# Decay matrices in four more places, first gram products together, inverse rows stored in one transfer

## The chip, the cores and the metric

The kernel runs on one core of one Trainium2 chip. The metric is the device time of one execution in microseconds (us); where several runs are given, their median. TensorE (PE) does the matrix products, VectorE (DVE), ScalarE (ACT) and GpSimd (POOL) the rest; SyncE (SP) issues nearly all DMA transfers. Each engine works through its own instructions in a fixed order.

## The reference

One layer of a diffusion backbone: a feed-forward block, then two mixers side by side (a neighbourhood attention and a bidirectional gated delta rule), then a second feed-forward block. The change lies in the delta rule, cut here to what matters:

```python
def gated_delta_chunks(q, k, v, g, beta, s0, with_output):
    # S_t = exp(g_t) (I - beta_t k_t k_t^T) S_{t-1} + beta_t k_t v_t^T,  o_t = S_t^T q_t
    k, v, g, beta = chunk(k), chunk(v), jnp.cumsum(chunk(g), axis=-1), chunk(beta)
    decay = jnp.exp(jnp.where(lower, g[..., :, None] - g[..., None, :], -jnp.inf))
    m = jnp.where(strict, jnp.einsum('...ik,...jk->...ij', k_beta, k) * decay, 0.0)
    uw = lax.linalg.triangular_solve(jnp.eye(GDN_CHUNK, dtype=m.dtype) + m, rhs,
                                     left_side=True, lower=True, unit_diagonal=True)
    ...
    def step(s, xc):
        v_new = xc[0] - jnp.einsum('...ck,...kv->...cv', xc[1], s)
        s_next = s * xc[3][..., None, None] + jnp.einsum('...ck,...cv->...kv', xc[2], v_new)
        return s_next, (jnp.einsum('...ck,...kv->...cv', xc[4], s)
                        + jnp.einsum('...cj,...jv->...cv', xc[5], v_new))
```

For each chunk of tokens there is a decay matrix `exp(g_i - g_j)` below the diagonal, the gram product of the keys times it, the inverse of one plus that matrix, and a scan that carries a state from chunk to chunk. The scores of queries against keys need the same decay matrix.

## The kernel before

The delta rule works on chunks of 128 tokens: two of context and four of latent tokens, forwards and backwards. A step `s` (0 to 5) handles one chunk of each direction, a pair `p` (0 or 1) two of the four heads, so one call handles four matrices at a time (index `m`). Steps go in groups `bi` of two: group 0 is steps 0 and 1 (context, no queries), group 1 steps 2 and 3, group 2 steps 4 and 5.

`gram(p, s, ...)` (lines 1106 to 1124) makes the decay matrices. Line 1110 loads the cumulated decays, broadcast over the partitions, into a tile `Dt`; line 1113 subtracts the column's value and adds the mask, one instruction a matrix; line 1114 takes the exponential on ACT. `Dt` is a tag with two buffers in the pool `gb_`, for twelve calls. Line 1119 makes `Bt`, gram product times decay times beta, and line 1120 stores it to DRAM (`bd`); where there are queries, line 1123 makes `At`. The products come from `products(p, s)`: group 0 takes them from PSUM (step 1 uses those of step 0), group 1 as well, and also stores them to DRAM (`kqd`, line 1094) for group 2, which loads them back (line 1098).

`base_inverse` (lines 1127 to 1153) inverts all 64 diagonal blocks of 32 x 32 of a group at once on DVE: lines 1138 to 1142 load the blocks from `bd` (two of four loads pass through `Ltr` and a copy on ACT), then 31 steps follow, each a product (line 1146, `bt`) and a sum (line 1147, `Xt`), each waiting for the one before. This is called the base chain below; there are three, one a group. A partition holds one block's columns of one parity. Lines 1150 to 1152 store the result to `rd` in four transfers. `inverse` (lines 1162 to 1226) loads it back as `T0` and `T1` (line 1168, two transfers), transposes on DVE (lines 1170, 1171) and joins the blocks to 128 x 128 inverses by small matrix products on PE (tile `pi`), with copies `Y`, `T6` and `Tt` on DVE and ACT between them. `scan_step` does a step of the scan; its products are in the tile `pc`, its sums on DVE are `r`, `vn`, `S`, and its output goes to one of the two tiles `oaccs`, written first at step 2.

What fills PE beside all this is the projection of the input: a fill is one column tile (24 matrix products of 128 x 512 into `pm`, lines 192 to 194), which needs its weights split on ACT (`wh`, line 137) and DVE (`wl`, line 139) and ends with a copy on ACT and a store (`spill`, lines 796 to 802). A fill comes in four pieces of six products. `turn(kind, i)` (line 1064) hands out a number of pieces from the table `RATE`, bound behind the last delta rule product: 2 after each gram of group 0, 3.9 after each product of group 1.

The program as written is not the order in which engines work: a scheduler with a simulated timeline places each engine's instructions, and `tc.issue_after(x)` keeps what it encloses behind instruction `x`. The sequence of the calls is this:

```python
    step(grams(0))
    base = grams(1)
    inv_of(0, 0)
    step(base, 4)
    inv_of(0, 1)
    step(base)
    scan_of(0, 0)
```

The attention's first loads (`att_load`: `qa`, `ka`, `kc`, `bias`, `va`, lines 1360 to 1367) go into the memory of `gb_` once that is closed, behind group 2's base chain in the program.

Of the kernel before, what the change touches and what calls it, by code (L numbers as in the profile page):

```python
# [13 lines left out]
ALU = mybir.AluOpType  # L14
# [4 lines left out]
P = 128  # L19
# [39 lines left out]
def body(ctx, tc, I, out, dbg=None):  # L59
    nc = tc.nc  # L60
    V, S, G, T = nc.vector, nc.scalar, nc.gpsimd, nc.tensor
# [15 lines left out]
    def tl(p, shape, tag, bufs=1, dt=F32):  # L77
        uid[0] += 1
        return p.tile(list(shape), dt, name=f"{tag}_{uid[0]}", tag=tag, bufs=bufs)
# [24 lines left out]
    marks = {}  # L104
# [461 lines left out]
    g = []  # L566
# [244 lines left out]
    beta = tl(gd, [P, 2, 6, 4], "beta")  # L811
# [252 lines left out]
    def turn(kind, i):  # L1064

        due[0] += RATE[kind][i]
        while due[0] >= 1:
            due[0] -= 1
            with tc.issue_after(last[0]):
                next(fills, None)  # L1070
# [9 lines left out]
    def products(p, s):  # L1080

        def one(n, a, o):
            if s == 1:
                return [kk01[p][:, m ^ 2] for m in range(4)]
            if s < 4:
                t = tl(pgq, [P, 4, P], "pq", 2)
                for m, (d, c, i) in enumerate(mats_of(s)):
                    mm(t[:, m, :], kT[2 * p + i][:, c], a[2 * p + i][:, c - o], start=True, stop=True)
                if s == 0:
                    kk01[p] = t  # L1090
                else:
                    u = tl(gb_, [P, 4, P], "kq", NKQ)
                    S.copy(u[:], t[:])
                    nc.sync.dma_start(kqd[n, s - 2, p], u[:].rearrange("p m c -> p (m c)"))
            else:
                t = tl(gb_, [P, 4, P], "kq", NKQ)
                for h in range(2):
                    nc.sync.dma_start(t[:, 2 * h:2 * h + 2].rearrange("p m c -> p (m c)"), kqd[n, 5 - s, p, :, 256 * (1 - h):256 * (2 - h)])
            return t
        yield one(0, kT, 0)  # L1100
        turn("g", s // 2)
        if s >= 2:
            yield one(1, qT, 2)
            turn("g", s // 2)

    def gram(p, s, bd, g):

        mats = mats_of(s)
        Dt = tl(gb_, [P, 4, P], "Dt", 2)
        nc.sync.dma_start(Dt[:], bass.AP(gcd.tensor, gcd.offset + (4 * s + 2 * p) * P, [[0, P], [24 * P, 2], [1, 2 * P]]))  # L1110
        for m, (d, c, i) in enumerate(mats):
            msk = cst[:, (C_MF if d == 0 else C_MB):][:, 0:P]
            V.scalar_tensor_tensor(Dt[:, m], Dt[:, m], gcum[:, d, s, 2 * p + i:2 * p + i + 1], msk, op0=ALU.subtract, op1=ALU.add)
        S.activation(Dt[:], Dt[:], AF.Exp)
        Bt, At = tl(gq, [P, 4, P], "Bt", NBT), None
        for n, t in enumerate(products(p, s)):
            if n == 0:
                for m, (d, c, i) in enumerate(mats):
                    V.scalar_tensor_tensor(Bt[:, m], t[m] if s == 1 else t[:, m], beta[:, d, s, 2 * p + i:2 * p + i + 1], Dt[:, m], op0=ALU.mult, op1=ALU.mult)
                nc.sync.dma_start(bass.AP(bd.tensor, bd.offset + g * MSTR, [[P, P], [4 * MSTR, 4], [1, P]]), Bt[:])  # L1120
            else:
                At = tl(gq, [P, 4, P], "At", NAT)
                V.tensor_tensor(At[:], t[:], Dt[:], ALU.mult)
        return Bt, At


    def base_inverse(bd, rd):


        L = tl(gb_, [P, 32, 32], "L")  # L1130
        tr = tl(gb_, [64, 32, 32], "Ltr")
        Xt = tl(gb_, [P, 16, 32], "Xt", 2)
        G.memset(Xt[:], 0.0)
        for q in range(4):
            G.memset(Xt[32 * q:32 * q + 32].rearrange("p c k -> p (c k)")[:, q % 2:512:34], 1.0)
        st = 32 * P + 32
        for q in range(4):
            dst = tr[32 * q:32 * q + 32] if q < 2 else L[32 * q:32 * q + 32]
            nc.sync.dma_start(dst, bass.AP(bd.tensor, bd.offset + (q // 2) * 8 * MSTR, [[st, 32], [P, 32], [1, 32]]))
        S.copy(L[0:64].rearrange("p r c -> p c r"), tr[:])  # L1140

        G.memset(L[:].rearrange("p r c -> p (r c)")[:, 0:1024:33], -1.0)
        for i in range(1, 32):
            c = (i + 1) // 2
            t = tl(gb_, [P, 16, 32], "bt")
            V.tensor_tensor(t[:, 0:c, 0:i + 1], L[:, i:i + 1, 0:i + 1].to_broadcast([P, c, i + 1]), Xt[:, 0:c, 0:i + 1], ALU.mult)
            V.tensor_reduce(Xt[:, 0:c, i], t[:, 0:c, 0:i + 1], AX, ALU.add, negate=True)
            if i % 4 == 0:
                yield
        for q in range(4):  # L1150
            nc.sync.dma_start(bass.AP(rd.tensor, rd.offset + (q // 2) * 32 * 1024 + (q % 2) * 32, [[1024, 32], [64, 16], [1, 32]]),
                              Xt[32 * q:32 * q + 32])
        yield


# [6 lines left out]
    def inverse(bi, st, rd, Bts):  # L1162


        T0 = tl(gq, [P, 8, 32], "T0", 2)
        T1 = tl(gq, [P, 8, 32], "T1", 2)
        for dst, d in ((T1, 0), (T0, 1)):
            nc.sync.dma_start(dst[:, 4 * d:4 * d + 4], bass.AP(rd.tensor, rd.offset + (st + 8 * d) * 4096, [[32, P], [2 * 4096, 4], [1, 32]]))
        fl = lambda t, m: t[:, m:m + 4].rearrange("p m c -> p (m c)")
        V.transpose(fl(T0, 0), fl(T1, 0))  # L1170
        V.transpose(fl(T1, 4), fl(T0, 4))
        blk = [slice(32 * b, 32 * b + 32) for b in range(4)]


        T6, Tt = T6s[inv_n[0] % NT6], Tts[inv_n[0] % NTT]
        inv_n[0] += 1
        sysm = lambda b: slice(0, 4) if b % 2 else slice(4, 8)
        bt = lambda k, b: Bts[k % 2][:, k // 2 + (0 if b else 2)]
        for b, r in enumerate(blk):
            o = 32 * (b % 2)  # L1180
            S.copy(T6[r, :, o:o + 32], T0[r])
            G.tensor_copy(Tt[r, :, 32 * b:32 * b + 32], T1[r])
        py = tl(pgq, [P, 4, 32], "pi", 2)
        for k in range(4):
            for b, r in enumerate(blk):
                q, m = blk[b ^ 1], k if b % 2 else 4 + k
                mm(py[r, k, :], bt(k, b % 2)[q, r], T0[q, m, :], start=True, stop=True, tile_position=(32 * (b ^ 1), 32 * b))
        turn("i", bi)
        Y = tl(gq, [P, 4, 32], "Y2", 2)
        V.tensor_copy(Y[:], py[:])  # L1190
        p0 = tl(pgq, [P, 4, 32], "pi", 2)
        p1 = tl(pgq, [P, 4, 32], "pi", 2)
        for k in range(4):
            for b, r in enumerate(blk):
                m = k if b % 2 else 4 + k
                mm(p0[r, k, :], T1[r, m, :], Y[r, k, :], start=True, stop=True, tile_position=(32 * b, 32 * b))
        turn("i", bi)
        for k in range(4):
            for b, r in enumerate(blk):
                m = k if b % 2 else 4 + k  # L1200
                mm(p1[blk[b ^ 1], k, :], Y[r, k, :], T1[r, m, :], start=True, stop=True, tile_position=(32 * b, 32 * (b ^ 1)))
        turn("i", bi)
        for b, r in enumerate(blk):
            o = 32 * ((b + 1) % 2)
            q = blk[b ^ 1]
            V.tensor_scalar(T6[r, sysm(b), o:o + 32], p0[r], -1.0, None, op0=ALU.mult)
            S.activation(Tt[q, sysm(b), r], p1[q], AF.Copy, scale=-1.0)

        hb = [slice(0, 64), slice(64, 128)]
        py = tl(pgq, [P, 4, 64], "pi", 2)  # L1210
        for k in range(4):
            for b in range(2):
                m = k if b else 4 + k
                mm(py[hb[b], k, :], bt(k, b)[hb[1 - b], hb[b]], T6[hb[1 - b], m, :], start=True, stop=True, tile_position=(64 * (1 - b), 64 * b))
        turn("i", bi)
        Y6 = tl(gq, [P, 4, 64], "Y6")
        V.tensor_copy(Y6[:], py[:])
        p1 = tl(pgq, [P, 4, 64], "pi", 2)
        for k in range(4):
            for b in range(2):  # L1220
                m = k if b else 4 + k
                mm(p1[hb[1 - b], k, :], Y6[hb[b], k, :], Tt[hb[b], m, hb[b]], start=True, stop=True, tile_position=(64 * b, 64 * (1 - b)))
        turn("i", bi)
        for b in range(2):
            S.activation(Tt[hb[1 - b], sysm(b), hb[b]], p1[hb[1 - b]], AF.Copy, scale=-1.0)
        return [[Tt[:, 4 * d + 2 * i + p] for d in range(2) for i in range(2)] for p in range(2)]
# [678 lines left out]
```

## Time and profile before

| | us |
|---|---|
| median of 3 runs | 1514.8 (1512.31, 1514.8, 1515.24) |
| the profiled execution | 1512.61 |
| its span, first to last instruction | 1510.8 |
| PE / DVE / ACT / POOL busy | 1441.6 / 1149.5 / 662.8 / 211.2 |

The views are read so. A row of the timeline gives the start in us, the duration, the engine, the line of the kernel, the operation, the tile written and the tiles read, the shape, the count and, in brackets, how long the engine sat idle before it and what ended that. SPq is SP's issue of a DMA. A row of the waits gives the total, the number of times and the longest. A row of the windows gives busy time (and count) of PE, its weight load, DVE, ACT and POOL, the clock granted to TensorE, the DMA share and GB/s. In matrix products of float32 the profile counts two rows for each instruction.

### The profile page before, as it was taken

What the parts mean: (1) busy time and instruction counts of PE and PEld (TensorE: products, weight loads), DVE (VectorE), ACT (ScalarE), POOL (GpSimd) and SP (SyncE); (2) the same over time, 40 slices, a digit from 0 to 9 for tenths busy, and PEclk for the clock granted to TensorE, in tenths of its full rate; (3) what the DMA queues carried; (4) which work ended last, traced back from release to release, by engine and by line L of the source; (5) the groups of instructions that cost most, each with busy time, mean ns of one, the idle gap of its engine ahead of it and who ended that gap; (6) DMA issues with size and microseconds to landing.
All of it is one profiled execution on the core that took longest, in us unless ns stands there. A gap on an engine that the chain in (4) does not pass through costs nothing.

```text
span 1510.8 us, 23895 instructions
## 1 busy us (share of the span) xinstructions
PE 1441.6 (95%) x9117; PEld 1262.9 (84%) x9117; DVE 1149.5 (76%) x1975; ACT 662.8 (44%) x1090; POOL 211.2 (14%) x262
## 2 busy tenths in 40 slices
PE   6998999999999989999996998989999999999997
PEld 4778989999997778889875777867778999998886
DVE  8787869999988665778677795567669699886626
ACT  5433524434333386555534334267526454444310
POOL 1000000000000110313201001333221022220001
PEclk9999999999999999999998999999999999999999
DMA  9677664445469444222576514274344143233732
GB/s 375 207 262 232 209 236 171 156 164 167 165 231 397 157 153 134 92 78 91 175 214 183 168 64 124 72 261 146 100 168 144 60 136 107 98 112 121 269 98 83
DMA packets 114948, 248.56 MB, mean 165 GB/s; under 512 B 35145, under 2 KB 50577, under 8 KB 114833
## 3 DMA queue, kind: packets, MB, share of 16 engines
q1 hardware_dynamic: 110192, 229.40, 45.4%
q0 software_dynamic: 3056, 12.33, 2.2%
q10 hardware_dynamic: 1586, 5.32, 0.9%
q8 instruction: 71, 1.16, 0.3%
q14 instruction: 43, 0.35, 0.1%
HBM read 215.50 MB, written 31.50 MB: 163 GB/s over the span
## 4 chain that ended last, share of the span: by engine, by line
PE 69%; DVE 13%; DMA 10%; issue 4%; ACT 3%; POOL 1%; SPq 1%; DVEq 0%; ACTq 0%; POOLq 0%
PE ps L211 15%; PE ps L533 4%; PE ps L535 4%; PE ps L534 4%; PE pm L192 4%; PE pm L193 4%; PE pm L194 4%; PE ps L193 3%; PE ps L192 3%; PE ps L1679 3%; PE ps L194 3%; PE ps L1680 3%; PE ps L1681 3%; PE pc L1049 2%; DVE wl L139 2%
## 5 line engine op out<-in xcount | busy, mean ns | idle before, releaser
L139 DVE TENSOR_TENSOR wl<-wr,wh 128x1024 fp32r<-128x1024 f32 (+1 forms) x184 | 226.8, 1238 | 119.2 <-ACT wh L137 119.0
L137 ACT CAST wh<-wr 128x1024 fp32r<-128x1024 f32 (+1 forms) x184 | 185.9, 1015 | 265.7 <-PE pm L193 60.1
L192 PE MATMUL pm<-uxh,wh 128*128 128x512 f32 x320 | 132.4, 414 | 1.0 <-ACT spill L798 1.0
L194 PE MATMUL pm<-uxh,wl 128*128 128x512 f32 x320 | 127.2, 397 | 0.3 <-DVE wl L139 0.3
L193 PE MATMUL pm<-uxl,wh 128*128 128x512 f32 x320 | 127.1, 397 | 0.0
L211 PE MATMUL ps<-wh,hx 128*128 128x512 f32 x352 | 96.1, 391 | 0.9 <-ACT wh L137 0.9
L211 PEld LDWEIGHTS ps<-wh,hx 128*128 128x128 f32 x352 | 65.9, 188 | 15.3 <-ACT wh L137 1.3
L280 DVE SCALAR_TENSOR_TENSOR adap<-wr,crow 128x1024 f32<-128x1024 f32 x61 | 74.6, 1223 | 2.3 <-DMA wr<-in_w_adaT_dram 1.7
L192 PE MATMUL ps<-uh,wh 128*128 128x256 f32 (+1 forms) x208 | 68.6, 331 | 5.0 <-ACT wh L137 5.0
L194 PEld LDWEIGHTS pm<-uxh,wl 128*128 128x128 f32 x320 | 61.1, 191 | 14.3 <-DVE wl L139 1.3
L192 PEld LDWEIGHTS pm<-uxh,wh 128*128 128x128 f32 x320 | 61.5, 192 | 12.6 <-ACT spill L798 1.4
L193 PEld LDWEIGHTS pm<-uxl,wh 128*128 128x128 f32 x320 | 61.4, 192 | 10.6
L114 POOL TENSOR_TENSOR rs<-ve,mhalf 128x1 f32<-128x1 f32 (+2 forms) x46 | 48.2, 1050 | 140.7 <-DVE ve L110 138.3
L193 PE MATMUL ps<-ul,wh 128*128 128x256 f32 (+1 forms) x208 | 67.5, 326 | 0.0
L194 PE MATMUL ps<-uh,wl 128*128 128x256 f32 (+1 forms) x208 | 66.6, 325 | 0.0
L193 PE MATMUL ps<-uxl,wh 128*128 128x256 f32 (+1 forms) x192 | 61.6, 324 | 2.1 <-DVE uxl L139 2.1
L192 PE MATMUL ps<-uxh,wh 128*128 128x256 f32 (+1 forms) x192 | 60.7, 323 | 1.6 <-ACT uxh L137 1.4
L194 PE MATMUL ps<-uxh,wl 128*128 128x256 f32 (+1 forms) x192 | 61.1, 321 | 0.0
L137 ACT CAST wh<-ra 128x1024 fp32r<-128x1024 f32 x31 | 32.6, 1053 | 58.1 <-PE ps L534 20.2
L533 PE MATMUL ps<-ur,wh 128*128 128x384 f32 x168 | 56.5, 336 | 0.0
L534 PE MATMUL ps<-ur,wh 128*128 128x384 f32 x168 | 56.4, 336 | 0.0
L533 PE MATMUL ps<-uh,wh 128*128 128x384 f32 x168 | 56.4, 336 | 0.0
(498 smaller groups left out, 4264.4 us busy)
## 6 DMA issues: line engine op xcount, KB each, us to landing
wr<-in_w_adaT_dram SPq DMA_DIRECT2D x64, 512.0 KB, 4.8
wr<-in_up_dram SPq DMA_DIRECT2D x56, 512.0 KB, 3.7
wr<-in_win_dram SPq DMA_DIRECT2D x52, 512.0 KB, 3.4
wr<-in_dn_dram SPq DMA_DIRECT2D x51, 512.0 KB, 4.0
ra<-in_up_dram SPq DMA_DIRECT2D x24, 512.0 KB, 4.2
rb<-in_up_dram SPq DMA_DIRECT2D x18, 512.0 KB, 3.3
ra<-in_w_adaT_dram SPq DMA_DIRECT2D x16, 512.0 KB, 5.0
wr<-in_w_o_dram SPq DMA_DIRECT2D x8, 512.0 KB, 4.5
```

What stands on the lines that cost most here:

```text
L114: G.tensor_tensor(rs[:], ve[:], mhalf[:, 0:n], ALU.pow)
L137: S.copy(hi, src)
L139: marks["lo"] = V.tensor_tensor(lo, src, hi.bitcast(F32), ALU.subtract).ins
L192: T.matmul(ps, a, uh[:, k, :], start=(k == 0), stop=False)
L193: T.matmul(ps, a, ul[:, k, :], start=False, stop=False)
L194: marks["mm"] = T.matmul(ps, b, uh[:, k, :], start=False, stop=(k == nk - 1)).ins
L211: T.matmul(banks[t][d][:, c0:c1], a[:, sl], b[:, d * 512 + c0:d * 512 + c1], start=first and j == 0, stop=last and j == 2)
L280: V.scalar_tensor_tensor(pr[:], raw[:], 1.0, crow, op0=ALU.mult, op1=ALU.mult, accum_out=col[:, c:c + 1])
L533: T.matmul(ps[:], a, mh, start=k == 0, stop=False)
L534: T.matmul(ps[:], a, ml, start=False, stop=False)
L535: T.matmul(ps[:], b, mh, start=False, stop=k == 3)
L1679: T.matmul(ps[:], a, uh[:, k], start=k == 0, stop=False)
```

## The change

Four things change. The decay matrices of pair 1 of group 0, and of both pairs of step 2, are made in quarters of the two `oaccs` tiles, which hold nothing until step 2's output; the two `Dt` buffers serve eight calls in place of twelve. The mask instructions of group 1 are bound behind the last `Bt` of group 0, those of group 2 behind the last `At` of group 1. The eight pieces of fill that stood two by two behind the grams of group 0 all stand behind the last of them. The inverse rows are stored in one transfer of 2 KB a partition, and each load of them becomes two, each to every second partition, since the two parities now lie apart.

```diff
         yield one(0, kT, 0)
-        turn("g", s // 2)
+        for _ in range(1 if s > 1 else 4 * s * p):
+            turn("g", s // 2)
...
+    def decay_place(s, p):
+
+        if s == 2 or s < 2 and p == 1:
+            a = 2 * (s == 2)
+            return oaccs[p if s == 2 else s][:, a:a + 2].rearrange("p a b c -> p (a b) c")
+        return tl(gb_, [P, 4, P], "Dt", 2)[:]
+
     def gram(p, s, bd, g):
 
         mats = mats_of(s)
-        Dt = tl(gb_, [P, 4, P], "Dt", 2)
+        Dt = decay_place(s, p)
...
-            V.scalar_tensor_tensor(Dt[:, m], Dt[:, m], gcum[:, d, s, 2 * p + i:2 * p + i + 1], msk, op0=ALU.subtract, op1=ALU.add)
+            with tc.issue_after(marks["At" if s > 3 else "Bt"]) if s > 1 else nullcontext():
+                V.scalar_tensor_tensor(Dt[:, m], Dt[:, m], gcum[:, d, s, 2 * p + i:2 * p + i + 1], msk, op0=ALU.subtract, op1=ALU.add)
...
-        for q in range(4):
-            nc.sync.dma_start(bass.AP(rd.tensor, rd.offset + (q // 2) * 32 * 1024 + (q % 2) * 32, [[1024, 32], [64, 16], [1, 32]]),
-                              Xt[32 * q:32 * q + 32])
+        nc.sync.dma_start(bass.AP(rd.tensor, rd.offset, [[512, P], [1, 512]]), Xt[:].rearrange("p c k -> p (c k)"))
...
         for dst, d in ((T1, 0), (T0, 1)):
-            nc.sync.dma_start(dst[:, 4 * d:4 * d + 4], bass.AP(rd.tensor, rd.offset + (st + 8 * d) * 4096, [[32, P], [2 * 4096, 4], [1, 32]]))
+            for q in range(2):
+                nc.sync.dma_start(dst[q:P:2, 4 * d:4 * d + 4], bass.AP(rd.tensor, rd.offset + (2 * d + q) * 16384 + st * 2048, [[32, 64], [2 * 2048, 4], [1, 32]]))
```

In the changed kernel the lines stand a little lower: the masks are line 1122, `Bt` 1128, `At` 1134, the base chain 1159 and 1160, the store 1163, the loads 1180.

DVE, from the first `Bt` of group 0 to the first step of the first base chain. `pq_7013` is the gram product of pair 0, `pq_7078` (before) and `pq_7043` (now) that of pair 1. Before:

```order
L1119 SCALAR_TENSOR_TENSOR Bt_7012<-pq_7013,beta_5207,Dt_7005 128x128 x4
L1119 SCALAR_TENSOR_TENSOR Bt_7049<-pq_7013,beta_5207,Dt_7042 128x128 x4
L1113 SCALAR_TENSOR_TENSOR Dt_7070<-Dt_7070,gcum_5208,cst_5205 128x128 x4
L139 TENSOR_TENSOR wl_7091<-wr_7088,wh_7090 128x1024
L1113 SCALAR_TENSOR_TENSOR Dt_7107<-Dt_7107,gcum_5208,cst_5205 128x128 x4
L1119 SCALAR_TENSOR_TENSOR Bt_7077<-pq_7078,beta_5207,Dt_7070 128x128 x4
L1119 SCALAR_TENSOR_TENSOR Bt_7114<-pq_7078,beta_5207,Dt_7107 128x128 x4
L139 TENSOR_TENSOR wl_7272<-wr_7269,wh_7271 128x1024
L1113 SCALAR_TENSOR_TENSOR Dt_7248<-Dt_7248,gcum_5208,cst_5205 128x128 x4
L1113 SCALAR_TENSOR_TENSOR Dt_7338<-Dt_7338,gcum_5208,cst_5205 128x128 x4
L1119 SCALAR_TENSOR_TENSOR Bt_7255<-pq_7256,beta_5207,Dt_7248 128x128 x4
L1146 TENSOR_TENSOR bt_7149<-L_7135,Xt_7137 128x2
```

Now, the same place; another `wl` and the first step of the chain are the two rows that follow:

```order
L1122 SCALAR_TENSOR_TENSOR oacc_1278_6939<-oacc_1278_6939,gcum_5208,cst_5205 128x128 x4
L1122 SCALAR_TENSOR_TENSOR oacc_1279_6940<-oacc_1279_6940,gcum_5208,cst_5205 128x128 x4
L139 TENSOR_TENSOR wl_7068<-wr_7065,wh_7067 128x1024
L1128 SCALAR_TENSOR_TENSOR Bt_7012<-pq_7013,beta_5207,Dt_7005 128x128 x4
L1128 SCALAR_TENSOR_TENSOR Bt_7030<-pq_7013,beta_5207,Dt_7023 128x128 x4
L1128 SCALAR_TENSOR_TENSOR Bt_7042<-pq_7043,beta_5207,oacc_1278_6939 128x128 x4
L1128 SCALAR_TENSOR_TENSOR Bt_7059<-pq_7043,beta_5207,oacc_1279_6940 128x128 x4
L1122 SCALAR_TENSOR_TENSOR oacc_1278_6939<-oacc_1278_6939,gcum_5208,cst_5205 128x128 x4
L1122 SCALAR_TENSOR_TENSOR oacc_1279_6940<-oacc_1279_6940,gcum_5208,cst_5205 128x128 x4
L1122 SCALAR_TENSOR_TENSOR Dt_7430<-Dt_7430,gcum_5208,cst_5205 128x128 x4
L139 TENSOR_TENSOR wl_7102<-wr_7099,wh_7101 128x1024
L1122 SCALAR_TENSOR_TENSOR Dt_7529<-Dt_7529,gcum_5208,cst_5205 128x128 x4
```

All masks of group 0 now stand ahead of its first `Bt`, and all masks of group 1 ahead of the base chain; before, two of group 1's stood ahead of it and two inside, with one of group 2.

PE, at the first inverse of group 1 (`T_1564` before, `T_1560` now). Before, its small products `pi` lie among those of the scan (`vn,ktail` and `S,kT`) and of a fill:

```order
L194 MATMUL pm_8358<-uxh_4690,wl_8225 128x512
L1049 MATMUL pi_8455<-Y_1567_8453,T_1565_8423 32x32 x13
L1049 MATMUL pc_8388<-vn_8381,ktail_8383 128x128 x4
L1049 MATMUL pi_8455<-Y_1567_8453,T_1565_8423 32x32 x3
L1049 MATMUL pi_8456<-T_1565_8423,Y_1567_8453 32x32 x16
L1049 MATMUL pc_8543<-S_1533_8304,kT_5221 128x128
L1049 MATMUL pc_8543<-S_1533_8304,kT_5222 128x128
```

Now all its products stand one behind the other, after that `S,kT` and the piece of fill that follows it:

```order
L1049 MATMUL pi_8432<-T_1560_8416,Bt_7249 32x32 x4
L1049 MATMUL pi_8432<-T_1560_8416,Bt_7338 32x32 x4
L1049 MATMUL pi_8451<-Y_1563_8449,T_1561_8417 32x32 x16
L1049 MATMUL pi_8452<-T_1561_8417,Y_1563_8449 32x32 x16
L1049 MATMUL pi_8493<-T_1275_6933,Bt_7249 64x64 x2
L1049 MATMUL pi_8493<-T_1275_6933,Bt_7338 64x64 x2
```

So the scan's products and the fill's, which lay between the stages of this inverse, now stand ahead of it.

SP, at the end of the third base chain. Before, the store in four, half of the loads of its result, the attention's loads, and the other half:

```order
L1151 DMA rd_1500_8137<-Xt_8311 512x1x32 x4
L1168 DMA T_1637_8860<-rd_1500_8137 128x4x32
L1168 DMA T_1677_9126<-rd_1500_8137 128x4x32
L1360 DMA qa_8659<-qad_5194 128x512
L1360 DMA ka_8664<-kad_5195 128x512
L1360 DMA kc_8669<-kcd_5190 128x256
L1365 DMA bias_8673<-in_na_bias_dram 128x3x512
L1367 DMA va_8675<-vad_5196 128x512
L1168 DMA T_1636_8859<-rd_1500_8137 128x4x32
L1168 DMA T_1676_9125<-rd_1500_8137 128x4x32
```

Now:

```order
L1163 DMA rd_1496_8131<-Xt_8305 128x512
L1372 DMA qa_8652<-qad_5194 128x512
L1372 DMA ka_8657<-kad_5195 128x512
L1372 DMA kc_8662<-kcd_5190 128x256
L1377 DMA bias_8666<-in_na_bias_dram 128x3x512
L1379 DMA va_8668<-vad_5196 128x512
L1180 DMA T_1633_8855<-rd_1496_8131 64x4x32 x2
L1180 DMA T_1632_8854<-rd_1496_8131 64x4x32 x2
L802 DMA kad_5195<-spill_8964 128x512
L1180 DMA T_1673_9123<-rd_1496_8131 64x4x32 x2
L1180 DMA T_1672_9122<-rd_1496_8131 64x4x32 x2
```

All loads of the result now stand behind the attention's five, and the store stands one store of a spill (`kad`) earlier in the queue.

More of the change, by code (lines that the diff above doesn't have):

```diff
@@ L1118, in gram @@
                 for m, (d, c, i) in enumerate(mats):
-                    V.scalar_tensor_tensor(Bt[:, m], t[m] if s == 1 else t[:, m], beta[:, d, s, 2 * p + i:2 * p + i + 1], Dt[:, m], op0=ALU.mult, op1=ALU.mult)
+                    b = V.scalar_tensor_tensor(Bt[:, m], t[m] if s == 1 else t[:, m], beta[:, d, s, 2 * p + i:2 * p + i + 1], Dt[:, m], op0=ALU.mult, op1=ALU.mult)
+                if s < 2:
+                    marks["Bt"] = b.ins
                 nc.sync.dma_start(bass.AP(bd.tensor, bd.offset + g * MSTR, [[P, P], [4 * MSTR, 4], [1, P]]), Bt[:])
@@ L1122, in gram @@
                 At = tl(gq, [P, 4, P], "At", NAT)
-                V.tensor_tensor(At[:], t[:], Dt[:], ALU.mult)
+                a = V.tensor_tensor(At[:], t[:], Dt[:], ALU.mult)
+                if s < 4:
+                    marks["At"] = a.ins
         return Bt, At
```

## The prediction

> **What bounds the kernel now.** I read the page first, then what PE waits for, then the windows around the waits.
>
> ```profile
> span 1510.8 us, 23895 instructions
> ```
>
> The execution took 1512.61 us, so 1.8 lie outside its span; the sum below is made against this execution. The waits of PE from 740 to 1000 us, where the delta rule lies:
>
> ```profile
> PE pi L1049 <- DMA T<-rd: 15.2, 3, 12.0
> PE pi L1049 <- DVE Y L1217: 4.2, 3, 2.6
> ...
> PE pm L192 <- ACT spill L798: 1.0, 1, 1.0
> ...
> PE pm L194 <- DVE wl L139: 0.3, 1, 0.3
> ```
>
> One wait stands out: 12.0 us, once, for the inverse rows coming back from DRAM. Its place is group 0's first inverse:
>
> ```profile
> 812.54 0.69 PE L1049 MATMUL pi<-T,Bt 32*32 32x32 f32 x32 [12.04 <-DMA T<-rd]
> ```
>
> PE had nothing left from 800.5 us on. The windows (PE, weight load, DVE, ACT, POOL, then the granted clock) show a second price:
>
> ```profile
> 800.00:812.50 12.50, 0.51 (x3) 0.08 (x1) 6.98 (x27) 2.58 (x2) 1.16 (x6) 0.72 0.88 208
> 812.50:817.00 4.50, 4.46 (x73) 3.33 (x74) 4.26 (x18) 2.87 (x6) 3.61 (x8) 0.64 0.29 92
> ...
> 844.00:850.00 6.00, 6.00 (x27) 4.73 (x24) 5.21 (x11) 0.76 (x2) 0.00 (x0) 0.51 0.82 265
> ...
> 925.00:930.00 5.00, 5.00 (x83) 4.26 (x82) 2.15 (x7) 2.71 (x9) 2.45 (x7) 0.66 0.01 2
> ```
>
> After each long wait the granted clock is low: 4.5 us at 0.64 cost 4.5 x 0.36 = 1.6 us, 6 us at 0.51 cost 2.9, 5 us at 0.66 cost 1.7. Elsewhere PE is busy, so a change here can win these waits and little more.
>
> What ended last ahead of 812.5 is the first base chain and the way to it. The rows of single lines on DVE, with the first and last start behind the durations: `Bt` of group 0, then the products of the first chain, then the sums of the first, second and third chain.
>
> ```profile
> L1119 DVE SCALAR_TENSOR_TENSOR Bt<-pq,beta,Dt x16: 342/344/347, 738.2 to 749.4; 128x128 f32<-128x128 f32 x16
> L1146 DVE TENSOR_TENSOR bt<-L,Xt x31: 160/293/682, 759.9 to 800.1; 128x2 f32<-128x2 f32 x1, 128x3 f32<-128x3 f32 x1, 128x8 f32<-128x8 f32 x1, 128x10 f32<-128x10 f32 x1
> L1147 DVE TENSOR_REDUCE Xt<-bt x31: 146/297/689, 760.8 to 800.8; 128x1 f32<-128x2 f32 x1, 128x1 f32<-128x3 f32 x1, 128x2 f32<-128x8 f32 x1, 128x2 f32<-128x10 f32 x1
> L1147 DVE TENSOR_REDUCE Xt<-bt x31: 155/297/689, 807.2 to 857.5; 128x1 f32<-128x2 f32 x1, 128x1 f32<-128x3 f32 x1, 128x2 f32<-128x8 f32 x1, 128x2 f32<-128x10 f32 x1
> L1147 DVE TENSOR_REDUCE Xt<-bt x31: 134/297/676, 861.9 to 909.2; 128x1 f32<-128x2 f32 x1, 128x1 f32<-128x3 f32 x1, 128x2 f32<-128x8 f32 x1, 128x2 f32<-128x10 f32 x1
> ```
>
> The first chain runs from 759.9 to 800.8 + 0.7 = 801.5: 41.6 us. What DVE did in it besides, and what it waited for (last column):
>
> ```profile
> L139 DVE TENSOR_TENSOR wl<-wr,wh 128x1024 fp32r<-128x1024 f32 x7 | 8.5, 1219 | 0.0
> L1119 DVE SCALAR_TENSOR_TENSOR Bt<-pq,beta,Dt 128x128 f32<-128x128 f32 x12 | 3.5, 344 | 0.0
> L1113 DVE SCALAR_TENSOR_TENSOR Dt<-Dt,gcum,cst 128x128 f32<-128x128 f32 x12 | 3.5, 348 | 4.6 <-DMA Dt<-gcd 4.6
> L1123 DVE TENSOR_TENSOR At<-pq,Dt 128x512 f32<-128x512 f32 x4 | 2.7, 684 | 0.0
> ```
>
> **The change, part by part.** *Start of the chain.* Before, pair 1's masks had to wait for a `Dt` buffer. Now their loads go out on SP behind this store:
>
> ```profile
> 733.59 0.38 SPq L1000 DMA_DIRECT2D vcd<-vcs  x1
> 735.99 1.05 PE L1049 MATMUL pq<-kT 128*128 128x128 f32 x8
> 749.77 4.42 DMA bd<-Bt
> ```
>
> How long transfers take from issue to landing (last column, 700 to 960 us):
>
> ```profile
> Dt<-gcd SPq DMA_DIRECT2D x12, 256.0 KB, 4.5
> bd<-Bt SPq DMA_DIRECT2D x12, 256.0 KB, 2.6
> ...
> Ltr<-bd SPq DMA_DIRECT2D x6, 128.0 KB, 3.9
> L<-bd SPq DMA_DIRECT2D x6, 128.0 KB, 3.5
> rd<-Xt SPq DMA_DIRECT2D x12, 64.0 KB, 2.2
> T<-rd SPq DMA_DIRECT2D x12, 64.0 KB, 3.2
> ```
>
> Issued at 734.0 and 734.5, the decays land at 738.5 and 739.0; two mask groups (3.5 / 12 x 4 = 1.2 us each) end at 740.9, the `wl` queued behind them at 742.1, sixteen `Bt` (4 x 1.2) at 746.9. The last ended at 749.4 + 0.35 = 749.8 before, and the chain began 10.1 later; so it begins at 757.0, 2.9 us sooner. The queue ahead of it on DVE (four mask groups, two `wl`: 7.2 us) ends at 754 and is covered by the store and the loads of the blocks. Side by side, the second product moves to 737; PE's sum of work is the same. The `wl` behind the masks is needed 24 products after 738, at 743.7; that leaves 1.6 us. If the decays land 3 us late, PE loses 1.4 there.
>
> *Length of the chain.* In the order one `wl`, three mask groups and one `At` leave it, and with the masks the wait for `Dt`: 1.2 + 3.5 + 0.7 + 4.6 = 10.0. It lasts 31.6 and ends at 788.6. Bounds: nothing gained in length, 798.6; as worked out, 788.6. I take the latter, since all its masks are then done; the gram products arrive at PE's old pace, ahead of the rows that use them.
>
> *Handing over.* SP's issues before:
>
> ```profile
> 802.90 4.11 SPq L1151 DMA_DIRECT2D rd<-Xt  x4
> ...
> 808.76 2.02 SPq L1168 DMA_DIRECT2D T<-rd  x4
> ```
>
> From the chain's end to 812.5 were 11 us: loads of the next blocks first, four stores (4.1 us to issue), four loads. Now the store stands ahead of those loads. One transfer of 256 KB is nearest to `bd<-Bt`, 2.6; then two stores in the queue (0.8), four issues (2.0) and 3.2 to land: 8.6. `T` is there at 797.2. Bounds of the store: 2.2 and 4.4 (the rows above). PE comes at 800.5 less the 1.3 us of waits for `spill` and `wl`, which hung on ACT and DVE held up by the masks: 799.2. So the 12.0 are gone with 2 us to spare. **Term A: -(12.0 + 1.3 + 1.6) = -14.9.**
>
> The Trainium skill speaks against one part here: "DMA: Bandwidth & Descriptors", section "Rules for kernel authors", has it that two transfers to disjoint halves of the partitions serialize and one over all 128 should be used. No run here shows such a pair yet; by this rule the halved loads would take another 3.2 us (the landing row), `T` would come at 800.4, and the sum would be 1.2 us poorer; by the rows, which show four loads issued in 2.0 us, nothing.
>
> *What is late next.* Term B: the second chain needs the last `Bt` of group 1, which PE's pace sets, then `Ltr` (3.9) behind the four loads of `T`. I put its start at 802 (bounds 799 and 807), 5 us sooner, while PE is 14.9 ahead. The next `Y` copy that PE waited 2.6 us for lies inside this chain. In the order it stood 75 rows behind the chain's first step and now stands 61; a row takes (857.5 - 807.2) / 93 = 0.54 us, so 14 rows are 7.6. The wait grows by 14.9 - 5 - 7.6 = 2.3. **B: +2** (bounds 0 and +5).
>
> Term C: at group 1's first inverse nothing lies between the stages any more, so two `Y`, `T6` and `Tt` are each waited for. The two shorter waits for `Y` are (4.2 - 2.6) / 2 = 0.8 each; four of about 0.8 to 1.2 make 4, where 2 were waited. **C: +2** (bounds 0 and +4).
>
> Term D: the third chain. The second ends between 850 (own length from 802) and 858 (as before); I take 856, nearer to the latter, since scan rows that wait for PE now stand among its last. The third begins some 4 us later, as before, and three `r`, an `S`, three `vn` and two `wl` have left it (3 x 1.2 + 1.2 + 3 x 0.7 + 2 x 1.2 = 9): 39 us in place of 48, to 899. Its loads:
>
> ```profile
> L1168 SPq DMA_DIRECT2D T<-rd x12: 370/451/501, 808.8 to 917.1; - x12
> DMA to landing us min/median/max: 2.0/3.2/6.9
> ```
>
> The last landed 6.9 us after 917, which is 13.8 after the chain. Now all four wait behind five loads of 1.66 MB: between 8 and 13.8, I take 10.5, so 909.5. PE came at 921.1, now 10.9 sooner and a scan turn (3 us) earlier in its order: 907. The wait is 2.5, as before (15.2 - 12.0 - 0.5 = 2.7). **D: 0** (bounds -4.4, wait and clock gone, and +3.5).
>
> Twelve more issues of loads and nine fewer of stores are 5 us of SP, hidden where SP waits; without that cover they delay the block loads, which is in B's bounds.
>
> **Sum.** -14.9 + 2 + 2 + 0 = -10.9: 1512.6 gives 1501.7. The three runs (1512.31, 1514.8, 1515.24) have a mean of 1514.1, 1.5 above the profiled one, so I say **1503**. The bounds of the terms together: -19.3 and -2.4, or 1495 and 1512. A measurement of this kernel can tell some 0.2% (3 us) from no change.
>
> **The rivals.** *Bigger:* the third wait goes too (D at -4.4) and B or C stays near 0: 1495 to 1498. For it: the third chain loses 9 us of other work. Against it: the loads now all queue behind the attention's. Chance 0.15.
>
> *Half:* the decays land late, or DVE falls behind, and the chain ends at 794 rather than 788.6: `T` comes at 802.6, a wait of 3.4 with its slow clock stays: 1507 to 1511. Chance 0.10.
>
> *Given back:* DVE is the bound. It is busy 6.98 of the 12.5 us in which PE waits, and in the next windows more; with B and C at their upper ends and D at +3.5 the time is 1512 to 1515. Chance 0.10.
>
> *Slower:* the third group's `T` behind the attention's loads. If the third chain still ends at 909.9, because its rows wait for PE, `T` comes at 920 to 924, PE at 907: a wait of 13 to 17 in place of 2.7, plus 2 of slow clock, +12 to +16 on -10.9: 1514 to 1520. It decides from a chain's end at about 909 on. Against it: the nine us that left it. Chance 0.05.
>
> That the change doesn't do what it says is little to fear: the masks' new places are in the order. The forecast (1498 to 1508) has 0.60. Faster by over 0.2%: 0.60 + 0.15 + 0.10 = 0.85; same 0.10; slower 0.05. From 1496 to 1512 some 0.8 lie.
>
> **What would show it.** Right: no wait of PE for `T` near 800; the first chain from 757 to 789 without a wait for `Dt`; one store of `rd` landing in under 3 us; the wait for `Y` near 830 at 3 to 6 us; the third chain ending near 899. Wrong: `T` after 800; the masks in `oaccs` waiting past 741; the third wait for `T` above 6 us.

## The result, and the profile after

| | before | changed | changed again |
|---|---|---|---|
| median, us | 1513.9 (1512.3 to 1515.2) | 1499.0 (1497.2 to 1504.6) | 1502.2 (1498.2 to 1503.9) |
| before in the same comparison | | 1513.9 | 1513.2 |
| ratio to before, 95% interval | | 0.9908 [0.988, 0.9937] | 0.9926 [0.9907, 0.9945] |
| profiled execution / span | 1512.6 / 1510.8 | 1499.2 / 1497.4 | 1502.0 / 1500.2 |

The changed kernel is 0.8% faster, some 11 to 15 us; 1503 had been forecast, in a range of 1496 to 1512. The second comparison was made last, as measure for the experiments.

The waits of PE from 720 to 960 us (total, times, longest), all of them:

```profile
PE pi L1049 <- DVE bt L1159: 4.4, 1, 4.4
PE pi L1049 <- DVE Y L1229: 3.7, 2, 2.4
PE pi L1049 <- DMA T<-rd: 2.9, 1, 2.9
PE pi L1049 <- DVE T L1218: 1.6, 2, 1.0
PE pi L1049 <- ACT Tt L1219: 1.2, 1, 1.2
PE pc L1049 <- DVE r L1260: 0.9, 1, 0.9
PE pm L194 <- DVE wl L139: 0.8, 1, 0.8
PE pi L1049 <- DVE Y L1202: 0.6, 1, 0.6
PE pc L1049 <- ACT Tt L1237: 0.3, 1, 0.3
```

The wait of 12.0 us for `T` is gone; the others, 11.5 us in all before, add up to 16.4 here. Where each arose is seen when the program is cut at the same places: at the first gram product, just behind the first inverse product (`pi<-T,Bt`) of groups 0, 1 and 2, at the transposes of the delta rule's output, and at the transposes behind the attention (line 148). That gives five stretches, the last of which is called the attention below. The windows of before (length, then busy time of PE, and in front of the last two columns the granted clock):

```profile
736.00:813.20 77.20, 63.86 (x348) 52.95 (x346) 54.96 (x164) 28.61 (x41) 1.62 (x8) 0.95 0.75 217
813.20:867.60 54.40, 50.98 (x454) 40.71 (x452) 43.27 (x115) 21.82 (x44) 3.78 (x10) 0.91 0.56 165
867.60:924.40 56.80, 51.53 (x540) 43.29 (x539) 46.73 (x127) 22.53 (x55) 7.25 (x12) 1.00 0.35 109
924.40:971.50 47.10, 45.49 (x477) 39.75 (x477) 26.23 (x63) 15.56 (x38) 10.21 (x18) 0.96 0.15 53
971.50:1131.10 159.60, 150.01 (x1047) 117.21 (x1045) 105.61 (x144) 84.97 (x173) 52.83 (x59) 0.98 0.49 166
```

And of the changed kernel:

```profile
735.40:799.90 64.50, 63.57 (x348) 53.31 (x347) 49.78 (x138) 26.91 (x40) 2.76 (x10) 1.00 0.74 227
799.90:871.00 71.10, 58.62 (x512) 47.32 (x510) 54.17 (x159) 27.92 (x55) 2.54 (x7) 0.95 0.60 167
871.00:916.40 45.40, 42.31 (x463) 36.27 (x464) 38.56 (x105) 20.33 (x50) 7.78 (x15) 0.89 0.33 105
916.40:962.10 45.70, 45.60 (x490) 40.13 (x489) 27.38 (x64) 13.59 (x32) 8.80 (x14) 1.00 0.22 71
962.10:1120.30 158.20, 150.95 (x1047) 117.95 (x1046) 103.76 (x145) 84.61 (x173) 52.73 (x59) 0.98 0.50 168
```

Length less busy time is PE's idle time: 13.3, 3.4, 5.3, 1.6 and 9.6 us before, 33.2 in all; 0.9, 12.5, 3.1, 0.1 and 7.2 now, 23.8. So **the first stretch won 12.4 us and the second gave 9.1 of them back**; the later ones won 6.0. That is 9.4 of the 10.2 us by which these 395.1 us became shorter; the other 3 us of the span lie before and behind, where the change does nothing. Those 3 us can't be counted as its gain: outside these stretches the profiled executions of all kernels here took from 1111 to 1119 us, whatever their edit.

### The profile page after: what moved, and what is told of

Same layout as the page of the kernel before. It is cut to its first block, busy times and chain, and to the rows that moved or that the text cites. A ratio compares the mean times of both kernels' runs of the same rounds, so it can differ in the third digit from the quotient of the medians.

```text
span 1497.4 us, 23915 instructions
## 1 busy us (share of the span) xinstructions
PE 1437.5 (96%) x9117; PEld 1260.5 (84%) x9117; DVE 1145.6 (77%) x1975; ACT 662.0 (44%) x1090; POOL 210.7 (14%) x262
## 4 chain that ended last, share of the span: by engine, by line
PE 70%; DVE 12%; DMA 9%; issue 3%; ACT 3%; POOL 1%; SPq 1%; DVEq 0%; POOLq 0%; ACTq 0%
PE ps L211 15%; PE pm L192 5%; PE ps L533 4%; PE ps L535 4%; PE ps L534 4%; PE pm L194 4%; PE pm L193 4%; PE ps L193 3%; PE ps L194 3%; PE ps L192 3%; PE ps L1691 3%; PE ps L1692 3%; PE ps L1693 3%; PE pc L1049 3%; DVE wl L139 2%
```

## Why the second stretch gives the time back

Two waits carry most of it, 7.3 us. The rows of PE at the first inverses of groups 0, 1 and 2:

```profile
799.21 0.45 PE L1049 MATMUL pi<-T,Bt 32*32 32x32 f32 x32
...
815.66 0.76 PE L1049 MATMUL pi<-Tt,Y 64*64 64x64 f32 x16 [4.41 <-DVE bt L1159]
...
870.33 0.45 PE L1049 MATMUL pi<-T,Bt 32*32 32x32 f32 x32 [2.89 <-DMA T<-rd]
...
915.68 0.45 PE L1049 MATMUL pi<-T,Bt 32*32 32x32 f32 x32
```

At 799.21 and at 915.68 nothing is waited for. The wait at 815.66 is put down to a row of the chain, but what it needs is `Y`, and DVE's rows ahead of it are these:

```profile
805.17 0.16 DVE L1159 TENSOR_TENSOR bt<-L,Xt 128x2 f32<-128x2 f32 x1 [4.09 <-POOL L L1155]
...
810.21 0.79 DVE L1134 TENSOR_TENSOR At<-kq,Dt 128x512 f32<-128x512 f32 x1 [0.84 <-DMA kq<-kqd]
810.92 0.37 DVE L1159 TENSOR_TENSOR bt<-L,Xt 128x21 f32<-128x21 f32 x1
812.74 0.61 DVE L1122 SCALAR_TENSOR_TENSOR Dt<-Dt,gcum,cst 128x128 f32<-128x128 f32 x2 [1.44 <-DMA Dt<-gcd]
...
814.20 0.87 DVE L1128 SCALAR_TENSOR_TENSOR Bt<-kq,beta,Dt 128x128 f32<-128x128 f32 x3
815.10 0.42 DVE L1229 COPY Y<-pi 128x256 f32<-128x256 f32 x1
```

DVE stood waiting, first 4.09 us for the blocks `L` of the second chain (POOL makes the last write into them), then for the loads of `kq` and of group 2's decays, with `Y` queued behind all of it. SP's queue shows why these came late (issue time in the second column):

```profile
790.10 0.32 SPq L1163 DMA_DIRECT2D rd<-Xt  x1
791.07 0.37 SPq L1131 DMA_DIRECT2D bd<-Bt  x1
...
792.62 2.65 SPq L1180 DMA_DIRECT2D T<-rd  x4
...
795.96 0.43 SPq L1152 DMA_DIRECT2D Ltr<-bd  x1
...
797.58 4.19 SPq L1152 DMA_DIRECT2D L<-bd  x2
801.81 1.41 SPq L1180 DMA_DIRECT2D T<-rd  x2
...
804.40 1.25 SPq L1180 DMA_DIRECT2D T<-rd  x2
805.69 2.02 SPq L1098 DMA_DIRECT2D kq<-kqd  x4
807.76 0.43 SPq L1118 DMA_DIRECT2D Dt<-gcd  x1
```

Two block loads take 4.2 us to issue and everything else follows them. The second wait, at 870.33, is the hand-over of the second chain. The sums of the first, the second and the third chain, with the start of the first and the last of them:

```profile
L1160 DVE TENSOR_REDUCE Xt<-bt x31: 150/297/689, 757.8 to 789.3; 128x1 f32<-128x2 f32 x1, 128x1 f32<-128x3 f32 x1, 128x2 f32<-128x8 f32 x1, 128x2 f32<-128x10 f32 x1
L1160 DVE TENSOR_REDUCE Xt<-bt x31: 113/288/672, 805.5 to 862.3; 128x1 f32<-128x2 f32 x1, 128x1 f32<-128x3 f32 x1, 128x2 f32<-128x8 f32 x1, 128x2 f32<-128x10 f32 x1
L1160 DVE TENSOR_REDUCE Xt<-bt x31: 146/297/690, 864.0 to 902.4; 128x1 f32<-128x2 f32 x1, 128x1 f32<-128x3 f32 x1, 128x2 f32<-128x8 f32 x1, 128x2 f32<-128x10 f32 x1
```

The first chain ended 11.5 us sooner (790.0), but the second began only 1.8 us sooner (805.2 for 807.0). Its blocks need the last key product of group 1, which PE makes at 786.4 (787.7 before), then `Bt`, a store, a load and a copy. The store was issued 3.7 us sooner (791.07, 794.79 before), and half of that was lost again: on SP the loads of the blocks (`Ltr`, 795.96 and 797.04; both from 797.04 on before) now stand behind the four half loads of `T`. The second chain ended 4.7 us later than before, and PE came sooner.

The third took 39.3 us in place of 48.2 and ended 6.8 us sooner, so group 2's inverse waits for nothing now. In it DVE was busy for 35.3 us, where it had been 43.9; the chain's own rows took 21.2 in both, so what shrank is the other work among them. The first two readings, late issues on SP and the late start of the second chain, were tried out below; the one of the third chain rests on these rows.

## Experiments

Each kernel was compared with before in five rounds. The four kernels with one part taken out and the repeat of the changed one ran on one chip, the others on two more: places alone, store alone, one load and fills in the inverse on the second, places and store and both with the keys first on the third. The changed kernel was not run on these two, so ratios from different chips are to be compared with care. The stretch is that from the first gram product to line 148, idle is PE's idle time in it, both from the windows of one profiled execution.

| kernel | ratio to before | first wait for `T` | stretch | idle |
|---|---|---|---|---|
| changed (again: 384.7, 23.6) | 0.9908 / 0.9926 | 0 | 384.9 | 23.8 |
| without the places | 0.9976 [0.9961, 0.9992] | 15.0 | 395.1 | 34.2 |
| without the binding | 0.9932 [0.9911, 0.9953] | 6.0 | 387.3 | 26.8 |
| with the old turns | 0.9930 [0.9909, 0.995] | 5.5 | 382.7 | 22.0 |
| with the old store and loads | 0.9950 [0.9931, 0.9969] | 0 | 390.7 | 30.4 |
| places alone | 0.9996 [0.998, 1.0012] | 6.8 | 397.6 | 35.7 |
| store alone | 1.0003 [0.9988, 1.0017] | 11.9 | 394.3 | 31.2 |
| places and store alone | 0.9990 [0.9974, 1.0005] | 6.7 | 386.5 | 27.9 |
| one load | 0.9922 [0.9904, 0.9941] | 0 | 385.2 | 23.6 |
| fills in the inverse | 1.0033 [1.0018, 1.0047] | 0 | 400.9 | 35.0 |
| keys first | 0.9957 [0.9935, 0.9978] | 0.2 | 391.3 | 26.6 |
| keys first, one load | 0.9952 [0.9934, 0.9969] | 0 | 382.6 | 22.7 |

**One part taken out of the change.** Without the places:

```diff
-        if s == 2 or s < 2 and p == 1:
-            a = 2 * (s == 2)
-            return oaccs[p if s == 2 else s][:, a:a + 2].rearrange("p a b c -> p (a b) c")
         return tl(gb_, [P, 4, P], "Dt", 2)[:]
```

> The changed kernel with every decay matrix back in the two Dt buffers; binding, turns, store and loads as changed. Theory 1 (the places make the lead, by clearing the first base chain of masks and of their wait): in the order two groups of masks and a wait for Dt lie inside the first chain again, so the chain lasts 37 to 42 us in place of 32, T lands at 802 to 810 in place of 796.9 and PE waits 3 to 10 us for it: 1503 to 1510 us. Rival 2 (side-by-side products, binding and one store make the lead): no wait for T near 800, 1497 to 1501 us.

The wait for `T` came back, at 15.0 us larger than the 12.0 of before; 1507.4 us. The first chain ran from 761.8 to 806.7, 45 us. Theory 1 holds in the chain and in the time; the wait was larger than it gave.

Without the binding:

```diff
-            with tc.issue_after(marks["At" if s > 3 else "Bt"]) if s > 1 else nullcontext():
+            with nullcontext():
```

> The changed kernel without the binding of the masks. In the order one group of masks moves ahead of the second half of the first Bt (1.1 us) and one group of group 2's masks into the first chain, nothing else near it. Theory 1: the first chain begins about 1 us later and lasts 1 us longer, which the 2 us between the landing of T (796.9) and PE's arrival (799.2) cover: 1497 to 1501 us. Rival 2 (the binding makes the lead): a wait for T of over 3 us near 800, 1503 us or more.

1502.1 us. Both were wrong in part: the wait of 6.0 us for `T` was there, as the rival said, and the time was hardly worse. The same with the old turns:

```diff
-        for _ in range(1 if s > 1 else 4 * s * p):
-            turn("g", s // 2)
+        turn("g", s // 2)
```

> The changed kernel with the fills of group 0 two by two again, so that the second gram product stands behind a piece of fill. Theory 1: Bt of pair 1 starts at 743.7 on DVE now and its product would be there at about 742 as before, so the chain moves by 0 to 1 us: 1497 to 1501 us. Rival 2 (the side-by-side products make the early start): the chain starts 3 us later or more, T lands past 800, 1501 to 1505 us.

The first chain started 3.2 us later and PE waited 5.5 us for `T`, as the rival said, but the time was 1499.7, as theory 1 said. In both, the waits of 1.0 and 4.4 us that follow in the changed kernel were absent: PE lost at 805 what it otherwise lost at 816. These two runs show the giving back most plainly: **whether PE waits 0 or 6 us for the first `T` does not change the end** by anything that ratios of 0.9932 and 0.9930 beside 0.9926 can tell.

With the old store and loads (lines 1151 and 1168 of before):

> The changed kernel with the inverse rows stored in four transfers and loaded whole, as before. Theory 1 (the hand-over is 7.1 us now and was 11): T lands near 800.8 for PE's arrival at 799.2, a wait of 1 to 3 us, and the second and third chain hand over 2 to 4 us later: 1501 to 1507 us. Rival 3 (the twelve more issues of halved loads cost SP more than the one store saves): faster, 1494 to 1498 us.

1503.5 us. There was no wait for the first `T` (PE came at 802.4 itself). In the profile the price lay later, with 11.0 us of idle time in the second stretch (12.5 in the changed kernel) and 6.4 in the third (3.1), and waits for `T` of 1.2 and 1.8; but the profiled execution, 1510.6 us, is the slowest of six (the others 1501.8 to 1504.5), so the place of the price is not certain. Theory 1 had the time and not the place.

**Parts alone.** `decay_place` in the kernel before:

> The kernel before with the four more places alone: no binding, old turns, four stores, whole loads. Theory 3 (places and one store are each worth about half): the wait for T near 805 is 4 to 8 us in place of 12, but later waits for Y and T grow: 1505 to 1510 us beside 1512 to 1514 for before. Rival (the places are all of it): 1498 to 1502 us.

The first wait fell from 12.0 to 6.8, as theory 3 had it, yet the time did not move. SP's queue in this kernel, at the end of the first chain:

```profile
796.92 0.93 SPq L1146 DMA_DIRECT2D Ltr<-bd  x2
800.95 2.69 SPq L1158 DMA_DIRECT2D rd<-Xt  x4
...
804.88 0.94 SPq L1175 DMA_DIRECT2D T<-rd  x2
805.88 2.18 SPq L1146 DMA_DIRECT2D L<-bd  x2
```

The chain ends earlier, so its four stores now stand ahead of half of the next chain's block loads (801.57 before, 805.88 here). The blocks were complete at 811.2 in place of 807.0. The second chain began later still, at 817.1, since the rows of group 0's inverse, an `At`, a `wl` and four masks stood ahead of it on DVE, and group 1's inverse waited 6.4 us for its `T`.

The one store and the halved loads in the kernel before:

> The kernel before with the one store and the halved loads alone. Theory 3: T after the first chain lands 2 to 4 us sooner (a wait of 8 to 10 us), the other hand-overs 1 to 4 us sooner: 1505 to 1510 us. Rival (the store is hidden wherever the chain is late anyway): 1511 to 1514 us.

The rival was right: no gain. The store stood behind the same block loads, the eight halved loads took 5.3 us to issue, and `T` was used at 812.80 in place of 812.54.

Places and store together, with neither binding nor side-by-side products:

> The changed kernel without the binding and with the old turns: the places and the one store with its halved loads alone. Theory 3 (these two carry the change, and each needs the other): 1496 to 1502 us. Rival (binding or side-by-side products carry a part that the other covered when one alone was taken out): 1503 to 1508 us.

1507.4 us against 1508.6: by the ratio the rival is right, and binding and turns, of which either can be missing, carry a part when both are. By the profile (stretch 386.5, idle 27.9) most of the gain is there; it is of an execution of 1504.3, at the low end of twelve (1504.2 to 1511.6). How much these two are worth together, 0.1% or 0.6%, and with it how much binding and turns add, stays open.

**What is late next.** One load over all 128 partitions:

```diff
...
-            for q in range(2):
-                nc.sync.dma_start(dst[q:P:2, 4 * d:4 * d + 4], bass.AP(rd.tensor, rd.offset + (2 * d + q) * 16384 + st * 2048, [[32, 64], [2 * 2048, 4], [1, 32]]))
+            nc.sync.dma_start(dst[:, 4 * d:4 * d + 4], bass.AP(rd.tensor, rd.offset + 2 * d * 16384 + st * 2048, [[32, 64], [16384, 2], [2 * 2048, 4], [1, 32]]))
```

> The changed kernel with each load of the inverse rows as one transfer over all 128 partitions from the new layout (12 issues in place of 24). Theory 2 (what is late after T at 797 is SP's queue: the loads of the blocks take 4.2 us to issue, and the second T pair, the kq loads and the decays that the Y copy stands behind on DVE follow them): twelve issues of 0.65 us less; the decays are issued 1.3 to 2.6 us sooner, the 4.4 us wait at 815.7 falls to 2 to 3, the wait for T at 870 from 2.9 to 0.3 to 1.5; 1494 to 1498 us. Rival 4 (DVE's own queue in the second chain is what is late, SP is not): the waits stay within 0.7 us, 1498 to 1501 us.

Theory 2's waits went further than it said: neither 4.4 at 816 nor 2.9 at 870 was left, and idle time in the second stretch fell from 12.5 to 5.4. Most of these 5.4 is a wait that was not there in the changed kernel: 3.58 us at 804.43 for the `Y` of the stage before, whose copy now stands behind the first rows of the second chain on DVE. The second chain began 2.3 us sooner than in the changed kernel (802.9), the third ended 6.6 us sooner (896.5). But the time, 1501.1 us, did not fall: the idle time of the third stretch rose to 4.8 and that in the attention to 10.8.

One piece of fill behind each stage of group 1's inverses (`"i": (1.5, 1, 0)`):

> The changed kernel with one piece of fill behind each stage of group 1's inverses (table RATE, i: 0 to 1); the pieces come from the attention stage behind the delta rule. Theory C (the stages of that inverse are uncovered latencies, 0.6 + 1.2 + 1.3 + 0.3 us and the slow clock behind them): these waits fall under 0.5 us each and the clock of 870 to 880 rises from 0.54; if the attention stage can spare the pieces, 1493 to 1497 us. Rival 5 (PE was only early: T at 870 and DVE set this place, and the attention stage lacks the pieces): the waits come back in the attention or at the next T, 1498 to 1504 us.

Rival 5, and worse than its price: 1517.5 us. The pieces were missing in the attention (1000 rows of matrix products there in place of 1047), which was idle for 13.6 us in place of 7.2; the wait for `T` at 870 grew to 4.6, and one stage of the inverse still waited 3.4 us for its `Y` (885.65).

The last two key products of group 1 ahead of the query products (`gram` hands back control behind the store of `Bt`, and makes `At` when it is called again):

```diff
...
+            if bi == 1 and j == 2:
+                continue
+            for h in (2, 3) if bi == 1 and j == 3 else (j,):
+                res[(bi, h)] = next(gen[h])
```

> The changed kernel with the last two key products of group 1 (step 3, pairs 0 and 1) side by side ahead of the two query products, so that the last Bt and with it the blocks of the second chain are ready some 11 us sooner. Theory D (the first chain's early end is given back because the second chain cannot start before PE has made group 1's last key product, 786.4, and its blocks have gone out and back, 805.2): the second chain starts between 791 and 798 in place of 805, ends near 850, PE's idle time between the first inverse of group 0 and that of group 1 falls from 12.5 to 4 to 8 us: 1490 to 1496 us. Rival 6 (DVE is the bound there: copies of Y and T6 queue behind the chain's rows wherever it starts): the idle time stays above 10 us or moves to the next T: 1497 to 1501 us.

> The kernel of the keys-first run with each load of the inverse rows as one transfer besides. Theory D with theory 2 (twelve issues less on SP bring the second T pair and the kq loads forward): 0 to 2 us less than the keys-first run, 1489 to 1495 us. If the second chain's start is not the bound: 1497 to 1501 us, as both alone.

The second and the third chain with the keys first:

```profile
L1161 DVE TENSOR_REDUCE Xt<-bt x31: 142/292/687, 794.8 to 850.1; 128x1 f32<-128x2 f32 x1, 128x1 f32<-128x3 f32 x1, 128x2 f32<-128x8 f32 x1, 128x2 f32<-128x10 f32 x1
L1161 DVE TENSOR_REDUCE Xt<-bt x31: 120/297/677, 855.4 to 904.0; 128x1 f32<-128x2 f32 x1, 128x1 f32<-128x3 f32 x1, 128x2 f32<-128x8 f32 x1, 128x2 f32<-128x10 f32 x1
```

The mechanism of theory D was there: start at 794.6, end at 850.8, idle time of the second stretch 8.0. Its price was not: 1502.1 us. The third chain began 8.5 us sooner and ended no sooner (904.7 against 903.1), since it lasted 49.5 us. The windows of this kernel show the idle time in the later stretches (55.80 - 50.24 = 5.6, 1.6, 9.1):

```profile
861.20:917.00 55.80, 50.24 (x494) 41.52 (x493) 42.86 (x118) 20.43 (x51) 7.41 (x12) 0.90 0.30 97
917.00:966.50 49.50, 47.90 (x518) 41.46 (x518) 27.41 (x65) 14.97 (x36) 10.12 (x18) 0.97 0.18 61
966.50:1125.60 159.10, 149.99 (x1047) 117.23 (x1045) 104.44 (x144) 84.84 (x173) 53.50 (x59) 0.98 0.49 167
```

In this third chain DVE was busy for 42.2 us, in that of the changed kernel for 35.3: the other work that had left it was back.

With one load besides, 1502.6: no more than each alone. So rival 6 fits better: DVE carries its three chains and what lies among them as one queue, and cured in one place, the wait comes up in the next. From the first chain's start to the third's end DVE is busy 120 us of 145 in the changed kernel, and in the other kernels 119 to 125 of 139 to 150. That DVE is the bound is argued, though, and not shown. No run gave DVE less to do, and it is idle for 19 to 27 us there. In the changed kernel it is 25, of which 20 are waits for data that come through DRAM: 8.6 us for the blocks `L`, 5.4 for `T`, 3.8 for the decays, 2.5 for `kq`. So the way of these data is a rival that stays open, though the kernel with one load, where DVE is idle least, was not faster.

**The changed kernel again.**

> The changed kernel itself, as measure for the runs with one part taken out: before had medians of 1513.9, 1511.9, 1511.9 and 1508.6 us in the four comparisons so far, so the parts are compared by their ratio to before. Theory 4 (all four parts are needed: 0.993 without the binding or with the old turns, 0.995 with the old store, 0.998 without the places, 0.999 with places and store alone): ratio 0.989 to 0.993. Rival 7 (the first comparison, of four runs, overstated it): 0.994 to 0.997, so that binding and side-by-side products are worth nothing one at a time.

0.9926, theory 4's end of the range. Its waits are the first profile's (4.7 at 815.8, 2.8 at 869.4). Beside it, on the same chip, taking out the places costs 0.5%, with intervals that lie apart (0.9961 to 0.9992 and 0.9907 to 0.9945). Taking out the store and its loads costs 0.2%, and there the intervals overlap (0.9931 to 0.9969), so this part is likely and not certain. Binding or turns alone are worth nothing that these runs can tell. No version tried was clearly faster than the change.

## Why the prediction came out, by its steps

- **Start of the chain, its length, the hand-over: right.** 757.6 for 757.0, 32.4 us for 31.6, end 790.0 for 788.6. The store landed in 2.0 to 2.5 us for 2.6, DVE took `T` at 796.9 for 797.2, PE came at 799.21 for 799.2. The decays were in the new places at 738.05 for 738.5. A wait of 0.85 us for `wl` at 751 had not been forecast. Term A counted 13.3 us of waits and 1.6 of slow clock; the idle time fell by 12.4, and the slow clock moved to the new wait (0.57 from 816 to 820 us).
- **The split loads.** The Trainium skill, "DMA: Bandwidth & Descriptors", section "Rules for kernel authors", would by the prediction's working have priced them at 1.2 us. The size agrees at the first hand-over: with halves DVE took the second tile at 796.88, with whole loads from the same layout at 795.82, both issued from 792.7 on, so the halves came 1.1 us later. The cause that the rows show is two more issues, 0.61 us for a half and 0.61 for a whole; the landings there were alike, 2.2 us for a half and 2.4 for a whole. It cost nothing here, since PE came 2.3 us after the tile; the times were 0.9926 and 0.9922 of before.
- **Term B: the step that failed.** "I put its start at 802" was 805.2, the end 862.9 and not 856, and for +2 the second stretch lost 9.1. The `Y` that B followed is the one that PE waited 2.58 us for at 843.58 before. Its wait did not grow to 3 to 6 us; it kept 2.4, at 835.94. What came was a wait of 4.4 at 816 for the `Y` of the same stage one inverse earlier, for which PE had not waited before (824.77) and which no term looked at. And the sum had no term for group 1's own wait for `T`, although by its own numbers `T` would have come at 864.6 and PE some 11 us before 866.9. That wait was 2.9 us, no more, because PE had already lost time on the way.
- **Term C: about right.** Behind group 1's first inverse product the stages waited 0.57, 1.18, 1.29 and 0.28 us, 3.3 in all for a forecast of 4; before, 1.05 and 0.47 for a forecast of 2. That is +1.8 for +2.
- **Term D: the chain right, the wait not.** 39.3 us for 39, end 903.1 for 899. PE, later than forecast by what the second stretch had lost, came at 915.7 and found `T` there: a gain of 3.7 us in the third and fourth stretch for a forecast 0, inside its bound of -4.4.
- **SP's issues.** 5 us more were forecast, hidden; for the stores and loads of the inverse rows they took 15.9 us in place of 14.2.
- **The sum** held because these errors had opposite signs, so that 1499.0 and 1502.2 lie this near to 1503 is in part luck. Some 5 us (2.3 in the attention, 3 outside the stretch) had no term at all; of the latter, before's own medians of 1508.6 to 1513.9 us in five comparisons, not all on one chip, show how far executions of one kernel lie apart.
- **The rivals.** "Given back", with 0.10, had the giving back, though not the time: 9.1 of the 12.4 us went that way. Its reason, DVE as the bound, fits and is not shown. The slower one did not come: the third chain ended before 909.

## What to carry to other kernels

When one long wait goes, ask of every later hand-over when its data would come and when the engine now would; a term for "the next wait" is not enough where three chains share one engine. An edit can be worth nothing alone (places 0.9996, store 1.0003) and still be missed when it is taken out of the whole (0.9976, 0.9950). Here the one brings a step forward; without the other its four stores then stand in the way of the next step's loads in one queue. Cut the program at the same instructions in both traces and compare idle time by stretch: it shows what waits by name hide.

## What was not expected of the hardware

Issuing is not always short: two block loads took 4.19 us behind two others (L<-bd, 797.58), and 0.93 in the keys-first kernel (790.87), where two `Ltr` loads had gone out 8 us before. These rows suggest that the time of an issue depends on what was issued just before it; that was not tried by itself.

A wait well under 3 us can already bring the slow clock. The windows around the wait of 2.38 us at 835.94:

```profile
832.00:836.00 4.00, 1.62 (x11) 1.25 (x10) 3.87 (x14) 3.33 (x7) 0.00 (x0) 1.00 0.20 80
836.00:840.00 4.00, 4.00 (x24) 3.29 (x25) 3.94 (x11) 0.76 (x2) 0.00 (x0) 0.58 0.64 204
840.00:844.00 4.00, 4.00 (x20) 3.28 (x20) 3.27 (x8) 0.25 (x1) 0.00 (x0) 1.00 0.98 250
```

The granted clock was 0.58 in the four us behind it: by estimate a price of 1.7 us (4 x 0.42), seven tenths of the wait again. The Trainium skill, "TensorE: Matmul & The Clock Gate", section "What's actually happening", has the clock fall after an idle window of about 3.4 us; here 2.4 us were enough. They are not always: in the kernel with places and store alone, a wait of 2.52 us ended at 841.01, and the granted clock was 1.00 in the four us behind it.
